# Small padding tiles in an encoder layer: every operand of TensorE at a multiple of 256 bytes

## The chip, the cores and the metric

One core of one Trainium2 chip. The metric is device time in microseconds (us) of one execution. The kernel before was timed three times; a fourth execution, under the hardware profiler, gave the trace that is read here.

## The reference

One encoder layer on x of 1024 rows by 1024 columns in float32, cut to what matters:

```python
h = rmsnorm(x, g_mix)
z = h @ w_in                                  # pooling channels | q | k | v
y_pool = pool_mixer(u_pool, w_pool_grp, pool_scale)
y_attn = diff_attention(q, k, v, ...)         # two softmax maps per head, block-causal chunks
gates = sigmoid(h @ w_gate + b_gate)
merged = gates[..., :D] * (y_pool @ w_branch_pool) + gates[..., D:] * (y_attn @ w_branch_attn)
x = x + merged @ w_out
h2 = rmsnorm(x, g_ffn)
x = x + square(relu(h2 @ w_up)) @ w_down
```

## The kernel before

All products run on TensorE. To keep float32 accuracy with a fast operand type, a float32 tile is split into a rounded high part and the rest (`split`, L127 on ScalarE, L128 on VectorE or GpSimd), and each product is three matmuls into the same PSUM bank, high by high, high by low and low by high (`mm3`, L133 to L135). Each matmul first loads a stationary operand of 128 columns (the profile's PEld), then streams a moving operand of 256, 384 or 512 columns. In the profile's names, `out<-in`, the first name behind the arrow is the moving operand and the second the stationary one: in `bp<-ypT,wbp`, ypT moves and wbp is loaded. The trace has 7601 matmuls: 7048 of `mm3` and of the score and sum products (L624, L625, L715, L716), which use the fast type, and 553 transposes against an identity tile (`identf`).

The work runs in stages. From about 30 to 700 us it makes q, k, v (`z`), scores (`sc`), transposed probabilities (`ta`), attention outputs (`po`), gates (`g`) and pooling channels (`u`), interleaved by a table of stages with steps (`ORDER`). From 700 to 910 us follow the branch products (`bp`, `ba`) and the output projection (`oX`, `oY`, `oZ`), from 910 to 1227 us the up projection (`X`, `Y`, `Z`, `W`), and to the end the down projection (`Da`, `Db`). The last three products are made by a scheme of seven half-size products (Strassen's), with sums on VectorE and GpSimd around them. TensorE takes its instructions in program order; each waits for semaphores of the engines that make its operands or free its bank.

SBUF tiles come from pools. A pool lays its tiles one behind the other in the order of first use, by bytes per partition, and the pools stand one behind the other; some pools (`side="right"`) are laid from the top end downwards. A tile of [128, n] float32 takes 4n bytes in each partition, rounded up to 32. The first tile of the kernel is `identf` (512 bytes), behind a reserved stretch and a few constants; then come `mhalf` (8 floats, 32 bytes), `ones` (512 bytes), `inv` and the small columns, and everything from the left end stands behind these. So the offset of a few small tiles within 256 bytes is passed on to all large tiles, which are multiples of 512 bytes. In the built program the matmuls' operands start, modulo 256 bytes, at:

| products | columns | matmuls | moving operand, before | stationary operand, before | both, after |
|---|---|---|---|---|---|
| `z` | 384 | 1536 | 96 | 96 | 0 |
| `g`, `u`, `bp`, `oX`, `oY`, `oZ`; `X`, `Z`, `W` over BT1, BT2, BT3, B22, BT4 | 512 | 2448 | 96 | 96 | 0 |
| `ba`; `X` and `Y` over B11, B21 | 512 | 768 | 224 | 96 | 0 |
| `Da`, `Db` | 512 | 1344 | 96 | 224 | 0 |
| `sc`, `po` over AT, `yp` | 256 to 512 | 888 | 224 | 224 | 0 |
| `po` over oqs | 256 | 64 | 160 | 160 | 0 |
| transposes `ta`, `tk`, `hps`, `hb` | 128 | 544 | 128 | 224 | 0 |
| nine small transposes (`trr`, `cols_ps`) | 128, 32 | 9 | 128 | 192, 128 | 0 moving; 32, 160 stationary |

Of the kernel before, what the change touches and what calls it, by code (L numbers as in the profile page):

```python
# [8 lines left out]
F32 = mybir.dt.float32  # L9
F32R = mybir.dt.float32r  # L10
# [7 lines left out]
P = 128  # L18
# [45 lines left out]
def encoder_kernel(  # L64
# [21 lines left out]
    nc = tc.nc  # L86
# [5 lines left out]
    const = ctx.enter_context(tc.tile_pool(name="const", bufs=1))  # L92
# [10 lines left out]
    fq = attn.enter_context(tc.tile_pool(name="fq", bufs=1))  # L103
    up = attn.enter_context(tc.tile_pool(name="up", bufs=N_U))
    ps_z = mix.enter_context(tc.tile_pool(name="ps_z", bufs=N_Z, space=PSUM))
    ps_f = mix.enter_context(tc.tile_pool(name="ps_f", bufs=N_F, space=PSUM))

    hcount = [0]

    def htile(shape, dt, name, th):  # L110
# [11 lines left out]
    def f(ap):  # L122
        return ap.bitcast(F32)

    def split(hi, lo, src, lo_eng=None):

        nc.scalar.copy(hi, src)  # L127
        return (lo_eng or nc.vector).tensor_tensor(lo, src, f(hi), op=ALU.subtract)  # L128

    def mm3(ps, lhs_hi, lhs_lo, rhs_hi, rhs_lo, first, last, more=False):  # L130

        kw = {"skip_group_check": True} if more else {}
        nc.tensor.matmul(ps, lhs_hi, rhs_hi, start=first, stop=False, **kw)  # L133
        nc.tensor.matmul(ps, lhs_hi, rhs_lo, start=False, stop=False, **kw)  # L134
        return nc.tensor.matmul(ps, lhs_lo, rhs_hi, start=False, stop=last, **kw)  # L135
# [103 lines left out]
        mp.append(m)  # L239


    identf = const.tile([P, P], F32, name="identf")
    make_identity(nc, identf)
    mhalf = const.tile([P, NT], F32, name="mhalf")
    nc.gpsimd.memset(mhalf, -0.5)
    ones = const.tile([P, P], F32R, name="ones")
    nc.gpsimd.memset(f(ones), 1.0)
    inv = const.tile([P, 16], F32, name="inv")
    for i in range(16):
        nc.gpsimd.memset(inv[:, i : i + 1], 1.0 / (i + 1))  # L250
# [1 line left out]
    cols = const.tile([P, 32], F32, name="cols")  # L252
    gs = const.tile([P, 1], F32, name="gs")
    zero = const.tile([P, 1], F32, name="zero")
    y_dram = dram.tile([D, S], F32, name="y_dram")
    r_dram = dram.tile([H, S], F32, name="r_dram")
    p_dram = dram.tile([POOLD, S], F32, name="p_dram")
# [150 lines left out]
    with ExitStack() as ph:  # L408
        sp = ph.enter_context(tc.tile_pool(name="sp", bufs=1))
# [4 lines left out]
        def s1(shape, dt, name, tag, bufs=1):  # L414
            return sp.tile(shape, dt, tag=tag, name=name, bufs=bufs)
# [274 lines left out]
        def stage_pv(h, p):  # L690
            V, views = KV[h][1], ATs.pop((h, p))[0]
            po = ps_o.tile([P, 512], F32, tag="o", name=f"po{h}_{p}")
            nkt = 2 * p + 2
            for kt in range(nkt):
                v = V[kt // 4]
                mm3(
                    po[:, 0:256], v[:, kt % 4, 0, :], v[:, kt % 4, 1, :],
                    views[kt][0], views[kt][1], kt == 0, kt == nkt - 1,
                )
                if kt % 2 and kt < nkt - 1:  # L700
                    yield
            oS = s1([P, 256], F32, f"oS{h}_{p}", "oS", 2)
            oq = s1([P, 256], F32, f"oq{h}_{p}", "oq")
            nc.scalar.activation(oq, po[:, 0:256], AF.Square)
            nc.scalar.copy(oS, po[:, 0:256])
            nc.scalar.dma_start(y_dram[h * P : (h + 1) * P, p * 256 : (p + 1) * 256], oS)
            oqs = s1([P, 2, 256], F32R, f"oqs{h}_{p}", "oqs")
            split(oqs[:, 0, :], oqs[:, 1, :], oq)
            st[h, p, "o"] = (po, oq, oqs)
            yield  # L710
# [34 lines left out]
        def stage(w, g):  # L745
            h, t = divmod(g, NT)
            if w == "A":
                if t == 0:
                    head_start(h)
                yield from stage_qkv(h, t)  # L750
            elif w == "B":
                yield from stage_prep(h, t)
            elif w == "C" and t % 2:
                yield from stage_qkT(h, t - 1)
            elif w == "D":
                yield from stage_scores(h, t)
            elif w == "E":
                yield from stage_aT(h, t)
            elif w == "F" and t % 2:
                yield from stage_pv(h, t // 2)  # L760
            elif w == "H" and t % 2:
                yield from stage_ssq(h, t // 2)
            elif w == "R" and t == NT - 1:
                yield from stage_norm(h)
            elif w == "W" and t == 0 and h:
                for kp in range(NK // 2):
                    load_w(h, kp)
                    split_w(h, kp, nc.gpsimd)
# [137 lines left out]
    def pool_of(stack, name, bufs, space=None, side=None):  # L906
        kw = {} if space is None else {"space": space}
        return stack.enter_context(
            tc.tile_pool(name=name, bufs=bufs, reuse_waits="tile", side=side, **kw)
        )  # L910

    hs = ctx.enter_context(ExitStack())
    norms = ExitStack()
    nb_pool = pool_of(hs, "nb", 4, side="right")
    pr1 = pool_of(hs, "pr1", N_R1, side="right")
    pr2 = [pool_of(hs, "pr20", 1, side="right")]
# [552 lines left out]
```

## Time and profile before

| | |
|---|---|
| median of 3 runs | 1545.42 us (1544.51 to 1545.88) |
| profiled execution | 1547.21 us, of which the span from first to last instruction 1545.4 us |
| granted TensorE clock | 1.000 |
| PE busy | 1527.3 us, 99% of the span, 7601 matmuls |
| PEld (stationary loads) busy | 1312.8 us, 85% |
| VectorE, ScalarE, GpSimd busy | 66%, 51%, 25% |
| DMA | 214.28 MB, mean 139 GB/s |

A matmul's record begins when it starts to fetch its moving operand and ends at a modelled time, so the records of consecutive matmuls overlap. What one matmul costs in a row of them is the time from its start to the start of the next, called its step below. A row of a group's answer gives first and last start and the count, from which the mean step follows; a window's count of matmuls in 100 us gives it too.

### The profile page before, as it was taken

The page shows a single profiled execution, that of the slowest core. Times are in us where ns is not written, and L with a number is a line of the kernel's source. Part 1 is how long each engine was busy: PE and PEld are TensorE (multiplying, and loading weights), DVE is VectorE, ACT ScalarE, POOL GpSimd, SP SyncE. Part 2 cuts the span into 40 slices and gives each one's busy share as a digit, 9 for nine tenths or more (in the row PEclk, how much of TensorE's full clock was granted, in tenths as well). Part 3 has the DMA queues.
Part 4 walks back from the last instruction along what each step waited for, and adds up shares of the span by engine and source line. Part 5 has one row for each costly group of instructions (what it writes and reads, how often), then busy time and mean ns, then how long its engine had stood idle before and what let it go on. Part 6 is the DMA issues. An engine that isn't in the chain of part 4 may idle for free.

```text
span 1545.4 us, 21680 instructions
## 1 busy us (share of the span) xinstructions
PE 1527.3 (99%) x7601; PEld 1312.8 (85%) x7601; DVE 1018.6 (66%) x2129; ACT 794.6 (51%) x1650; POOL 390.6 (25%) x469
## 2 busy tenths in 40 slices
PE   6999999999999999999999999999999999999999
PEld 6999999999999999888888887888888788888887
DVE  6777767677777778642635799667656677546662
ACT  6656555555555655544633477556555633333331
POOL 5434242434344343219637510000000000000000
PEclk9999999999999999999999999999999999999999
DMA  7112111111212121349736534555433899437650
GB/s 228 39 57 65 39 60 51 57 52 44 65 40 68 34 86 52 113 136 382 252 109 198 196 124 134 166 183 164 150 124 108 306 348 349 153 123 261 222 177 28
DMA packets 168568, 214.28 MB, mean 139 GB/s; under 512 B 10157, under 2 KB 104074, under 8 KB 168458
## 3 DMA queue, kind: packets, MB, share of 16 engines
q1 hardware_dynamic: 151050, 185.58, 36.2%
q10 hardware_dynamic: 17408, 27.30, 4.9%
q8 instruction: 60, 0.98, 0.3%
q14 instruction: 50, 0.41, 0.1%
HBM read 155.14 MB, written 57.70 MB: 138 GB/s over the span
## 4 chain that ended last, share of the span: by engine, by line
PE 93%; DVE 2%; DMA 2%; POOL 1%; ACT 1%; SPq 1%; issue 1%; ACTq 0%; POOLq 0%; DVEq 0%
PE z L135 6%; PE z L134 6%; PE z L133 6%; PE Da L134 4%; PE Da L135 4%; PE g L135 4%; PE Da L133 4%; PE g L134 4%; PE g L133 4%; PE Db L133 3%; PE Db L135 3%; PE Db L134 3%; PE X L133 3%; PE X L135 3%; PE X L134 3%; PE sc L624 2%
## 5 line engine op out<-in xcount | busy, mean ns | idle before, releaser
L135 PE MATMUL z<-wqkv,hT 128*128 128x384 f32 x512 | 173.8, 340 | 1.3 <-DVE hT L128 1.3
L133 PE MATMUL z<-wqkv,hT 128*128 128x384 f32 x512 | 174.8, 342 | 0.0
L134 PE MATMUL z<-wqkv,hT 128*128 128x384 f32 x512 | 174.2, 340 | 0.0
L635 ACT ACTIVATE s<-s,nm 128x256 f32<-128x256 f32 (+7 forms) x128 | 99.5, 778 | 73.8 <-DVE nm L627 70.7
L264 POOL TENSOR_TENSOR ms<-ms,mhalf 128x4 f32<-128x4 f32 x64 | 65.9, 1029 | 209.0 <-DVE ms L263 193.8
L133 PE MATMUL g<-hT,fwgate 128*128 128x512 f32 x256 | 101.0, 394 | 0.0
L135 PE MATMUL g<-hT,fwgate 128*128 128x512 f32 x256 | 100.6, 393 | 0.0
L134 PE MATMUL g<-hT,fwgate 128*128 128x512 f32 x256 | 100.5, 392 | 0.0
L135 PEld LDWEIGHTS z<-wqkv,hT 128*128 128x128 f32 x512 | 96.8, 189 | 3.3 <-DVE hT L128 2.4
L133 PEld LDWEIGHTS z<-wqkv,hT 128*128 128x128 f32 x512 | 96.9, 189 | 2.8 <-ACT hT L127 0.4
L134 PEld LDWEIGHTS z<-wqkv,hT 128*128 128x128 f32 x512 | 96.9, 189 | 1.7
L627 DVE CUSTOM_DVE_ANT_0 s<-sc,dist 128x512 f32<-128x512 f32 (+3 forms) x128 | 74.3, 585 | 23.5 <-PE sc L625 22.5
L624 PE MATMUL sc<-K,Q 128*128 128x512 f32 (+2 forms) x192 | 67.3, 356 | 0.4 <-DVE nm L627 0.4
L128 POOL TENSOR_TENSOR wqkv<-rqkv,wqkv 128x384 fp32r<-128x384 f32 x60 | 63.2, 1069 | 14.1 <-ACT wqkv L127 10.9
L625 PE MATMUL sc<-K,Q 128*128 128x512 f32 (+2 forms) x192 | 66.1, 349 | 0.0
L128 DVE TENSOR_TENSOR AS<-s,AS 128x512 fp32r<-128x512 f32 x64 | 43.4, 687 | 33.1 <-ACT AS L127 33.0
L128 POOL TENSOR_TENSOR fwgate<-frgate,fwgate 128x512 fp32r<-128x512 f32 x32 | 42.7, 1336 | 63.4 <-ACT fwgate L127 63.4
L135 PEld LDWEIGHTS g<-hT,fwgate 128*128 128x128 f32 x256 | 48.1, 188 | 9.6
L133 PEld LDWEIGHTS g<-hT,fwgate 128*128 128x128 f32 x256 | 48.1, 188 | 9.1 <-ACT go L382 0.2
L134 PEld LDWEIGHTS g<-hT,fwgate 128*128 128x128 f32 x256 | 48.1, 188 | 8.8
L135 PE MATMUL ba<-yT,wba 128*128 128x512 f32 x128 | 50.4, 395 | 0.0
L133 PE MATMUL ba<-yT,wba 128*128 128x512 f32 x128 | 50.4, 395 | 0.0
(458 smaller groups left out, 4595.4 us busy)
## 6 DMA issues: line engine op xcount, KB each, us to landing
wd<-in_w_down_dram SPq DMA_DIRECT2D x56, 512.0 KB, 5.4
wu<-in_w_up_dram SPq DMA_DIRECT2D x32, 512.0 KB, 5.1
udS<-us SPq DMA_DIRECT2D x64, 256.0 KB, 3.6
ur<-udS SPq DMA_DIRECT2D x32, 512.0 KB, 3.3
rqkv<-in_w_in_dram SPq DMA_DIRECT2D x64, 192.0 KB, 2.9
ur<-ud SPq DMA_DIRECT2D x24, 512.0 KB, 6.1
frgate<-in_w_gate_dram SPq DMA_DIRECT2D x32, 256.0 KB, 2.7
g_dram<-go ACTq DMA_DIRECT2D x32, 256.0 KB, 2.8
```

Of the source, the lines that this page charges most:

```text
L128: return (lo_eng or nc.vector).tensor_tensor(lo, src, f(hi), op=ALU.subtract)
L133: nc.tensor.matmul(ps, lhs_hi, rhs_hi, start=first, stop=False, **kw)
L134: nc.tensor.matmul(ps, lhs_hi, rhs_lo, start=False, stop=False, **kw)
L135: return nc.tensor.matmul(ps, lhs_lo, rhs_hi, start=False, stop=last, **kw)
L264: nc.gpsimd.tensor_tensor(dst, dst, mhalf[:, :n], op=ALU.pow)
L624: nc.tensor.matmul(dst, Q[:, i, 0, :], rhs, start=True, stop=False)
L625: nc.tensor.matmul(dst, Q[:, i, 1, :], rhs, start=False, stop=True)
L627: nc.vector.tensor_tensor_reduce(out=s[i][:, c : c + w], in0=sc[:, 0:w], in1=dist[:, o0 + c : o0 + c + w], scale=2.0 ** -(h + 1), scalar=B ...
L635: nc.scalar.activation(s[i][:, 0:n], s[i][:, 0:n], AF.Exp, bias=last, scale=-1.0, accum_out=Z[:, i, t : t + 1])
```

## The change

Five tiles that nothing reads or writes are allocated, to shift what stands behind them, and two small constants change places, so that the 512-byte tile comes ahead of the 32-byte one. The pads take 128 and 32 bytes in the pool of constants, 128 bytes in `fq` (the pool of the attention stage's wide tiles), 64 bytes in `sp` (its small tiles, at the place where `sp`'s tile list reaches the operands of the sum product), and 224 bytes at the right end, ahead of the pools of the output projection, the up and the down projection. After it 7592 of the 7601 matmuls have both operands at a multiple of 256 bytes, as the last column of the table shows. The tiles of the other engines and of the DMAs move by the same shifts: on VectorE 3769 operand places of the program were at 32 modulo 64 bytes and 934 at 0; after it 887 and 3816.

```diff
@@ encoder_kernel, the pools
+    def pad(pool_, n):
+        pool_.tile([P, n], F32, tag=f"pad{n}", name=f"pad{n}")
+
+    pad(fq, 32)
     hcount = [0]
@@ the constants
+    pad(const, 32)
     identf = const.tile([P, P], F32, name="identf")
     make_identity(nc, identf)
+    ones = const.tile([P, P], F32R, name="ones")
+    nc.gpsimd.memset(f(ones), 1.0)
     mhalf = const.tile([P, NT], F32, name="mhalf")
     nc.gpsimd.memset(mhalf, -0.5)
-    ones = const.tile([P, P], F32R, name="ones")
-    nc.gpsimd.memset(f(ones), 1.0)
@@
     zero = const.tile([P, 1], F32, name="zero")
+    pad(const, 8)
@@ stage_pv
             nc.scalar.dma_start(y_dram[h * P : (h + 1) * P, p * 256 : (p + 1) * 256], oS)
+            if not (h or p):
+                pad(sp, 16)
@@ after the attention pools are closed
     norms = ExitStack()
+    pad(pool_of(ctx, "edge", 1, side="right"), 56)
     nb_pool = pool_of(hs, "nb", 4, side="right")
```

The one place where instructions move is GpSimd's start, where it fills the constants. Before:

```order
masks.py:197 MEMSET identf 128x128
L245 MEMSET mhalf 128x8
L247 MEMSET ones 128x128
L250 MEMSET inv 128x1
masks.py:199 ISA
```

And now, with the lines numbered by the changed file:

```order
masks.py:197 MEMSET identf 128x128
L250 MEMSET ones 128x128
L252 MEMSET mhalf 128x8
L255 MEMSET inv 128x1
masks.py:199 ISA
```

The two fills have changed places, and GpSimd's first use of `mhalf` waits for a count of 3 instead of 2 on its own semaphore. TensorE, VectorE, ScalarE and the DMA queue of SyncE have the same instructions in the same order with the same waits as before.

## The prediction

> **What bounds the kernel now.** I read the page's first part, then TensorE's waits, then windows of 100 us.
>
> ```profile
> PE 1527.3 (99%) x7601; PEld 1312.8 (85%) x7601; DVE 1018.6 (66%) x2129; ACT 794.6 (51%) x1650; POOL 390.6 (25%) x469
> ```
>
> From all waits of TensorE (engine, line, releaser; us, times, longest), the four longest:
>
> ```profile
> PE hps L290 <- DVE hn L285: 9.5, 2, 9.0
> PE z L135 <- DVE hT L128: 1.3, 2, 1.1
> PE hps L290 <- DVE hT L128: 0.8, 1, 0.8
> PE oX L133 <- DVE mp L799: 0.6, 1, 0.6
> ```
>
> These make 12 us, all but 0.6 of it at the first tiles (`hps` and the first `z`); after that no other engine holds TensorE up. So the time is the sum of the steps from one matmul to the next, and what each step costs is the question. The windows (busy us and instructions of PE, PEld, DVE, ACT, POOL where present; clock; DMA share; GB/s):
>
> ```profile
> 100.00:200.00 100.00, 100.00 (x590) 92.61 (x589) 70.81 (x214) 58.26 (x147) 34.15 (x47) 1.00 0.17 52
> 700.00:800.00 100.00, 100.00 (x435) 81.47 (x435) 43.70 (x50) 48.85 (x77) 68.83 (x48) 1.00 0.76 267
> 1000.00:1100.00 100.00, 100.00 (x439) 82.04 (x439) 68.17 (x108) 60.20 (x109) 0.00 (x0) 1.00 0.52 167
> 1200.00:1300.00 100.00, 99.28 (x428) 79.96 (x427) 68.68 (x71) 46.77 (x58) 0.00 (x0) 1.00 0.92 329
> 1300.00:1400.00 100.00, 100.00 (x430) 80.43 (x430) 55.40 (x52) 36.04 (x36) 0.00 (x0) 1.00 0.49 170
> ```
>
> The clock is granted in full throughout. From 1300 to 1400 us only matmuls of 512 columns run, 430 of them: a step of 232.6 ns. The same shape has another step elsewhere, and that is the first thing to explain. From the answers on the tiles `bp` and `ba` (duration ns min/median/max, first and last start in us):
>
> ```profile
> L133 PE MATMUL bp<-ypT,wbp x64: 389/389/389, 700.0 to 742.9; 128*128 128x512 f32 x64
> L135 PE MATMUL bp<-ypT,wbp x64: 389/389/389, 700.5 to 743.3; 128*128 128x512 f32 x64
> L133 PE MATMUL ba<-yT,wba x128: 392/392/398, 743.6 to 832.5; 128*128 128x512 f32 x128
> L135 PE MATMUL ba<-yT,wba x128: 392/398/398, 744.0 to 832.9; 128*128 128x512 f32 x128
> ```
>
> `bp` is 192 matmuls from 700.0 to 743.3 us: 43.3/191 = 226.7 ns a step. `ba` is 384 from 743.6 to 832.9: 89.3/383 = 233.2 ns. Shape, clock and types are equal, and neither waits. What differs in the program is where the operands start: `bp` has both at 96 modulo 256 bytes, `ba` has its moving operand at 224 and its stationary one at 96. In the list of groups nearly every one with equal offsets outside the attention stage has a mean of 389 to 392 ns, and every one with offsets 128 apart 394 to 398:
>
> ```profile
> L135 PE MATMUL oX<-wo,A 128*128 128x512 f32 x64 | 24.9, 389 | 0.0
> L133 PE MATMUL Z<-B22h,AS 128*128 128x512 f32 x64 | 24.9, 389 | 0.0
> L133 PE MATMUL Y<-B21h,A 128*128 128x512 f32 x64 | 25.4, 397 | 0.0
> L133 PE MATMUL Da<-w_2h,u_2h 128*128 128x512 f32 x32 | 12.6, 395 | 0.0
> ```
>
> So addresses reach TensorE's pace. I take that as shown; how far it goes is not.
>
> **The change, part by part.** Nothing is added to any engine: the pads are never touched. GpSimd's two fills change places ahead of the first transposes, which wait 9 us for VectorE's `hn` anyway (the row above); that costs nothing, and without this cover it would be the time of a fill of 8 floats.
>
> First term, the unequal offsets. They belong to 384 (`ba`), 384 (`X` and `Y` over B11 and B21), 768 (`Da`) and 576 (`Db`) matmuls, 2112 together. After the change all are equal, as `bp`'s are now: 2112 × (233.2 − 226.7) = 13.7 us. TensorE's queue is the path, so it counts in full.
>
> Second term, what is left in `bp`'s step. To split it I need other widths; from the timeline of PE, a run of `po` with 256 columns, its first and last, 22 steps apart, and a run of `z` with 384, 8 steps up to the first `g`:
>
> ```profile
> 674.18 0.28 PE L134 MATMUL po<-AT_0l,V 128*128 128x256 f32 x1
> ...
> 676.81 0.28 PE L135 MATMUL po<-AT_4h,V 128*128 128x256 f32 x1
> ```
>
> ```profile
> 319.97 0.34 PE L134 MATMUL z<-wqkv,hT 128*128 128x384 f32 x1
> ...
> 321.36 0.39 PE L133 MATMUL g<-hT,fwgate 128*128 128x512 f32 x1
> ```
>
> 2.63/22 = 119.5 ns at 256 columns, 1.39/8 = 173.8 at 384, 226.7 at 512. From 256 to 512 columns the step grows by 107.2 ns, 0.419 ns a column; taken off, 12 to 13 ns remain at all three widths. So each matmul of the fast type carries about 13 ns that don't depend on its length, while both its operands start at an odd multiple of 32 bytes. Is that the offset's doing, or the price of passing from one matmul to the next? The nearest rows in which the moving operand starts at a multiple of 128 bytes are the transposes, whose identity is at 128:
>
> ```profile
> 123.50 1.03 PE L680 MATMUL ta<-identf,s 128*128 128x128 f32 x8
> 124.29 0.36 PE L624 MATMUL sc<-K,Q 128*128 128x256 f32 x1
> 124.49 0.28 PE L625 MATMUL sc<-K,Q 128*128 128x256 f32 x1
> 124.61 0.28 PE L624 MATMUL sc<-K,Q 128*128 128x256 f32 x1
> ```
>
> The record after the transposes begins early, so I count to the one behind it: from 123.50 to 124.49 lie eight transposes and one `sc`, whose own step is 120 (124.49 to 124.61): 870/8 = 109 ns each. If a column of their slower type takes twice 0.419 ns, which I can only infer, 128 take 107 and 2 ns remain, not 13, although their stationary operand starts at 224. That speaks for the moving operand's offset. Nor does the stationary load's size matter: behind the last head a transpose with 8 stationary columns (its load takes 83 ns where others take 188) is loaded under a `g`, and that `g`'s step stays 220 to 230 ns:
>
> ```profile
> L736 PEld LDWEIGHTS trr<-identf,r x8: 83/83/84, 144.7 to 690.4; 128*8 128x8 f32 x8
> ...
> 690.38 0.39 PE L133 MATMUL g<-hT,fwgate 128*128 128x512 f32 x1
> 690.60 0.27 PE L736 MATMUL trr<-identf,r 128*8 128x128 f32 x1
> ```
>
> The bounds of this term are 0 (a fixed price) and 13 ns (all of it the offset). I take 11, the remainder less the transposes' 2, since theirs is the only row with an aligned moving operand: 7048 × 11 = 77.5 us.
>
> The Trainium skill ("TensorE: Matmul & The Clock Gate", section "Back-to-back issue gap") gives a warm step of N/2.4 + 2.5 ns. That is 215.8 at 512 columns where this trace has 226.7 at best, and 10.9 × 7048 would be 76.8 us.
>
> Third term, new waits. The other engines' work does not shrink, unless their tiles' new places help them, which no row shows; their waits cost TensorE 12 us at most now, so I price that at 0 to a few us either way. Where TensorE's cover is thin I take a share back. DMA is 92% busy from 1200 to 1300 us (the row above): 428 matmuls there lose up to 17.5 ns each, 7.5 us, and 92.5 us leave no slack for 92 us of DMA: I take 3. Two stretches of the chain that ended last lie off TensorE, each from the first to the last of its pieces (start us, length):
>
> ```profile
> 819.36 0.63 ACT wo L127
> ...
> 865.78 0.61 DVE mp L799
> 912.01 0.87 ACT y L1021 x3
> ...
> 940.56 0.61 DVE BT1l L128
> ```
>
> That is 47 and 29 us of other engines' and DMA work which just meets TensorE. If TensorE covers them 6% faster, 3 and 2 us appear as waits. In the attention stage VectorE is 71 us busy of 100; 94 would still hold that, and I allow 2. Together 10 us.
>
> The sum for the profiled execution: 1547.2 − 13.7 − 77.5 + 10 = 1466.0 us. The median of the timed runs is 1.8 below that execution: 1464.
>
> **The rivals.** (a) Only equal offsets count, and the 13 ns are the price of passing to the next matmul: the term of 77.5 is nothing. For it: the remainder is the same for `z` at offset 96 and `po` at 224, and a constant needs no memory to explain it. Against it: the transposes. 1547.2 − 13.7 − 1.8 = 1532.
>
> (b) Half of the remainder goes, because one of the two operands' offsets makes a part of it: 38.8 + 13.7 less 5 of waits, 1498.
>
> (c) No change: the steps of `bp` and `ba` differ by something else in their stages, such as DMA or evacuation. The groups above, the same in four stages, are against it. 1545.4. The Trainium skill ("SBUF — State Buffer", section "Specifications (TRN2)") has lines of 16 bytes, and by that rule 32, 96, 160 and 224 are starts of lines already, so nothing would be gained; `ba` against `bp` does not agree.
>
> (d) Slower: with every operand at offset 0, the moving stream, the next stationary load and the other engines' accesses start in the same place of the memory at the same time, and meet. The dearest step in these rows is `ba`'s slower record, 398 against `bp`'s 389. If all steps go there, 4936 matmuls pay 9 ns and 2112 pay 2.5 more than their mean: 44.4 + 5.3 = 49.7 us, 1595. It decides once the mean step over all 7048 rises by 2 ns (13.7/7048) above `bp`'s level. Against it: equal offsets are the cheaper case in every group above.
>
> **How the numbers follow.** The forecast (the remainder gone to 9 to 13 ns) 0.56; (b) 0.13; (a) 0.16; (c) 0.08; (d) 0.07. The likeliest case alone runs from 1450 (13 ns, 7048 × 13 = 91.6 instead of 77.5) to 1482 (9 ns and a few more waits). The range goes up to 1538, (a) with half of its gain, and so takes in (a) and (b); it leaves out (c), (d) and a little below 1450, under 2 in 10. A difference of 0.2%, 3 us, is about what the three runs' spread can tell. All of the forecast, (a) and (b) are faster by more: 0.85; (c) is the same: 0.08; (d) slower: 0.07.
>
> **What would show it.** Right: the count of matmuls from a window inside the down projection rises from 430 to some 460 in 100 us and that of `bp`'s steps falls to about 216 ns; `bp` and `ba` have one mean; `po` near 109 and `z` near 163; transposes stay at 109. Wrong in the second term: `bp` stays at 226.7 with `ba` joining it (a), or stops between 217 and 225 (b). Wrong in the third: PE's waits grow past 20 us, at `oX` behind `wo`, at `Da` behind `w_0h` or `w_0l`, or anywhere in the attention stage. Wrong altogether: `bp`'s step above 227.

## The result, and the profile after

| | before | after |
|---|---|---|
| median of five runs, same chip | 1545.42 us | 1532.73 us |
| ratio | | 0.9924, interval 0.9905 to 0.9942 |
| profiled execution (span) | 1547.21 (1545.4) us | 1532.49 (1530.7) us |

The change makes the kernel 12.7 us faster. I had forecast 81. The number is that of rival (a), 1532, in which only the difference of the two offsets counts and nothing of the 13 ns goes.

The page's first part of the changed kernel, and the window inside the down projection:

```profile
PE 1513.4 (99%) x7601; PEld 1314.4 (86%) x7601; DVE 1027.9 (67%) x2129; ACT 794.7 (52%) x1650; POOL 390.1 (25%) x469
1300.00:1400.00 100.00, 100.00 (x443) 82.85 (x442) 56.82 (x54) 36.39 (x37) 0.00 (x0) 1.00 0.49 170
```

TensorE is still the bound, and 443 matmuls stand in the window where 430 stood. A window counts about two records that only reach into it, so I read steps from a window as 100 us over the count less two, good to about 0.5 ns: 226.8 ns here, 233.6 before. The answers on `bp` and `ba` (lines 137 to 139 are 133 to 135 of before):

```profile
L137 PE MATMUL bp<-ypT,wbp x64: 388/390/390, 699.8 to 742.6; 128*128 128x512 f32 x64
L139 PE MATMUL bp<-ypT,wbp x64: 388/390/390, 700.2 to 743.1; 128*128 128x512 f32 x64
L137 PE MATMUL ba<-yT,wba x128: 388/390/390, 743.3 to 829.6; 128*128 128x512 f32 x128
L139 PE MATMUL ba<-yT,wba x128: 388/390/390, 743.7 to 830.1; 128*128 128x512 f32 x128
```

`bp` keeps its step: 43.3 us over 191, 226.7 ns, although both its operands moved from 96 to 0. `ba` fell to it: 86.8 over 383, 226.6 ns. The groups of other stages, from the list, show the same meeting at one mean:

```profile
L139 PE MATMUL oX<-wo,A 128*128 128x512 f32 x64 | 24.9, 389 | 0.0
L137 PE MATMUL Z<-B22h,AS 128*128 128x512 f32 x64 | 24.9, 389 | 0.0
L137 PE MATMUL Y<-B21h,A 128*128 128x512 f32 x64 | 25.1, 392 | 0.0
L137 PE MATMUL Da<-w_2h,u_2h 128*128 128x512 f32 x32 | 12.5, 389 | 0.0
L686 PE MATMUL ta<-identf,s 128*128 128x128 f32 x288 | 44.9, 272 | 0.0
```

`Y` and `Da` had 397 and 395; the transposes' 272 is unchanged. So is their step. The same eight of them in the changed kernel:

```profile
123.32 1.04 PE L686 MATMUL ta<-identf,s 128*128 128x128 f32 x8
124.11 0.36 PE L630 MATMUL sc<-K,Q 128*128 128x256 f32 x1
124.31 0.28 PE L631 MATMUL sc<-K,Q 128*128 128x256 f32 x1
124.43 0.28 PE L630 MATMUL sc<-K,Q 128*128 128x256 f32 x1
```

From 123.32 to 124.31, less one `sc` of 120 ns, are 870 ns, 109 each as before, although their operands were 96 bytes apart (128 and 224) and now both start at 0. Behind the first tiles no wait of TensorE is longer than 0.8 us; its four longest are:

```profile
PE hps L296 <- DVE hn L291: 8.9, 1, 8.9
PE hps L296 <- DVE hT L132: 1.2, 1, 1.2
PE X L137 <- ACT BT2h L131: 0.8, 1, 0.8
PE z L139 <- DVE hT L132: 0.7, 2, 0.5
```

So the gain is where the prediction's first term put it, and the second term's 77.5 us are absent. The experiments ask two things: is it the difference of the offsets alone that counts, and whose are the 13 ns that stayed?

### The profile page after: what moved, and what is told of

It reads as the page before. It is cut to its first block, busy times and chain, and to the rows that moved or that the text cites. A ratio compares the mean times of both kernels' runs of the same rounds, so it can differ in the third digit from the quotient of the medians.

```text
span 1530.7 us, 21680 instructions
## 1 busy us (share of the span) xinstructions
PE 1513.4 (99%) x7601; PEld 1314.4 (86%) x7601; DVE 1027.9 (67%) x2129; ACT 794.7 (52%) x1650; POOL 390.1 (25%) x469
## 4 chain that ended last, share of the span: by engine, by line
PE 97%; DVE 2%; DMA 0%; issue 0%; ACT 0%; SPq 0%; POOL 0%; ACTq 0%; POOLq 0%
PE z L139 6%; PE z L137 6%; PE z L138 6%; PE g L139 4%; PE g L138 4%; PE g L137 4%; PE Da L138 4%; PE Da L139 4%; PE Da L137 4%; PE Db L137 3%; PE Db L139 3%; PE Db L138 3%; PE X L139 3%; PE X L137 3%; PE X L138 3%; PE sc L630 2%
```

## Experiments

**One pad, no multiple of 256.** The kernel before with one line more (`pad` is the helper of the changed kernel):

```diff
+    pad(pool_of(ctx, "edge", 1, side="right"), 32)
     nb_pool = pool_of(hs, "nb", 4, side="right")
```

> The kernel before with one pad alone: 128 bytes at the right end, so that the tiles there move from 224 to 96 modulo 256 and meet the others' 96. 1728 matmuls (X and Y over B11 and B21, Da, Db) become equal at 96; ba's 384 stay 128 bytes apart; nothing is at a multiple of 256. If only the difference of the two offsets counts: 1545.4 - 1728 x 6.5 ns = 1534, Da and Db at 226.7 ns a step, ba at 233. If a start at a multiple of 256 is what pays: no change, 1545, Da and Db at 233.

Measured: 1535.25 us (median of four runs) against 1545.05 of the kernel before beside it, ratio 0.9938 (0.9921 to 0.9954). Its window and its `ba`:

```profile
1300.00:1400.00 100.00, 100.00 (x443) 82.80 (x442) 56.51 (x54) 37.04 (x37) 0.00 (x0) 1.00 0.52 172
L136 PE MATMUL ba<-yT,wba x128: 392/392/398, 743.5 to 832.4; 128*128 128x512 f32 x128
L138 PE MATMUL ba<-yT,wba x128: 392/398/398, 744.0 to 832.9; 128*128 128x512 f32 x128
```

The down projection has the step of the changed kernel with both operands at 96; `ba`, left apart, keeps its 233 ns (89.4 over 383).

**All equal at 96.** The same with a second pad of 128 bytes, the changed kernel's own ahead of the attention tiles:

```diff
+    pad(fq, 32)
...
+    pad(pool_of(ctx, "edge", 1, side="right"), 32)
     nb_pool = pool_of(hs, "nb", 4, side="right")
```

> The kernel before with two pads of 128 bytes, at the right end and ahead of the attention stage's tiles: every matmul of the fast type but the 64 sum products has both operands at 96 modulo 256, none at 0. If only the difference counts: the same time as the changed kernel, 1532 to 1533, all steps of 512 columns at 226.7. If the multiple of 256 has a share of its own: slower than the changed kernel by that share, up to 1545.

Measured: 1533.54 us (median of four runs) against 1545.05, ratio 0.9926 (0.9911 to 0.9940); the changed kernel's 0.9924 lies in this interval. `ba`:

```profile
L137 PE MATMUL ba<-yT,wba x128: 389/389/389, 743.5 to 829.8; 128*128 128x512 f32 x128
L139 PE MATMUL ba<-yT,wba x128: 389/389/389, 743.9 to 830.3; 128*128 128x512 f32 x128
```

86.8 over 383 again. A multiple of 256 has no share of its own that can be measured; two pads do what five and an exchange do.

**Other distances.** The changed kernel with the right end's pad made shorter, so that one operand of 1728 matmuls moves away from 0: by 64 bytes (`edge` of 40 floats), 32 (48) and 128 (24).

```diff
-    pad(pool_of(ctx, "edge", 1, side="right"), 56)
+    pad(pool_of(ctx, "edge", 1, side="right"), 40)
```

> The changed kernel with 160 bytes instead of 224 at the right end: 1728 matmuls (X and Y over B11 and B21, Da, Db) have operands 64 bytes apart instead of equal. If any difference modulo 256 costs what 128 bytes did: Da and Db at 233 ns a step, 1544. If only a difference of 128 bytes collides: 226.7 as now, 1532.5. If two equal starts are themselves a collision and make the 13 ns remainder: below 226.7, down to 216, and 1514.

> The changed kernel with 192 bytes instead of 224 at the right end: Da, Db and X, Y over B11, B21 have operands 32 bytes apart. If any unequal pair pays 6.5 ns: Da and Db at 233, 1544. If the price goes by the 64-byte or 128-byte place: 32 bytes apart costs nothing, 227 and 1532.5.

> The changed kernel with 96 bytes instead of 224 at the right end: Da, Db and X, Y over B11, B21 are again 128 bytes apart, now at 0 and 128 instead of 96 and 224. If only the difference counts: 233.3 ns a step in alternating steps near 229 and 238, as in the kernel before, 1544. If a start at 128 is as good as one at 0: 226.7 and 1532.5.

Measured, one run each: 1547.23, 1545.15 and 1544.80 us. The windows, in the order 64, 32, 128; first:

```profile
1300.00:1400.00 100.00, 100.00 (x430) 80.12 (x430) 55.66 (x52) 36.04 (x36) 0.00 (x0) 1.00 0.50 171
```

then:

```profile
1300.00:1400.00 100.00, 100.00 (x430) 80.50 (x429) 54.25 (x50) 35.26 (x36) 0.00 (x0) 1.00 0.49 167
```

and:

```profile
1300.00:1400.00 100.00, 100.00 (x432) 81.04 (x432) 54.83 (x51) 35.63 (x37) 0.00 (x0) 1.00 0.49 170
```

Steps of 233.6, 233.6 and 232.6 ns. Every distance tried costs 5.8 to 6.8 ns on average over the 226.8 of equal offsets, whether 32, 64 or 128 bytes, and the hope that some distance takes the 13 ns away fell with it. A start at 128 is hardly better than one at 32 or 64 when the other operand is at 0, and the two alternating steps expected there did not come back: start to start, the trace has steps spread from 228 to 241. That the period is 256 bytes and not 512 follows from `ba` in the changed kernel: there its moving operand and the next stationary one lie an odd multiple of 256 bytes apart in the built program, at 226.6 ns.

**The 2-byte type.** The changed kernel with the down projection's parts in bfloat16, in tiles of the old size, so that addresses stay; first run once, then timed.

```diff
-            hi, lo = (pool_.tile([P, 2, 512], F32R, tag="op", name=f"{n}{j}_{q}{x}") for x in "hl")
-            split(hi, lo, src, dve)
+            hi, lo = (
+                pool_.tile([P, 2, 1024], mybir.dt.bfloat16, tag="op", name=f"{n}{j}_{q}{x}")[:, :, 0:512] for x in "hl"
+            )
+            nc.scalar.copy(hi, src)
+            nc.vector.tensor_tensor(lo, src, hi, op=ALU.subtract)
```

> The changed kernel with the down projection's operands (Da, Db) in a 2-byte type at the same addresses (high and low parts rounded to bfloat16, so the result is coarser). If the 13 ns remainder is the price of passing from any matmul to the next: steps stay at 226.7 ns, 443 matmuls in 100 us. If it belongs to the 4-byte type: steps near 216, 1344 x 11 ns = 15 us less, 1518.

> The kernel of the first look at the 2-byte type again, now timed: the changed kernel with Da's and Db's operands in bfloat16. By that look 1518, 15 us or 1.0% below the changed kernel; if the look was chance, 1532.

Measured: 1518.17 us in the single run; timed, 1518.09 us (median of four runs) against 1545.22 of the kernel before, ratio 0.9822 (0.9805 to 0.9838), faster than both kernels, at the price of coarser parts. The timed kernel's windows, and its longest wait in the down projection:

```profile
1200.00:1300.00 100.00, 99.07 (x454) 52.43 (x454) 75.92 (x76) 46.80 (x57) 0.00 (x0) 1.00 0.96 355
1300.00:1400.00 100.00, 100.00 (x466) 45.30 (x464) 58.91 (x56) 39.37 (x40) 0.00 (x0) 1.00 0.55 186
PE Da L137 <- ACT w_0h L1376: 0.7, 1, 0.7
```

100/464 is 215.5 ns a step: 11 of the remainder's 12 to 13 ns go with the type, at the same addresses and 512 columns. The Trainium skill's formula ("TensorE: Matmul & The Clock Gate", section "Back-to-back issue gap") gives 215.8 for it and agrees; for the 4-byte type this trace is 11 ns above the formula. That section calls the formula the gap of an isolated matmul and gives about 131 ns for a stream of loads and matmuls at 512 columns; no run here comes near that (215.5 is the lowest), though every matmul here has its own load. The first window shows a DMA share of 0.96 with 454 matmuls in it, 438 in the changed kernel's, and TensorE's longest wait in the down projection is 0.7 us.

The same exchange in the kernel before, where the operands are 128 bytes apart:

> The kernel before with the down projection's operands in the 2-byte type at the same addresses, 128 bytes apart (96 and 224; the result is coarser). If unequal offsets cost a 2-byte stream too: Da and Db near 222 ns a step. If the 2-byte type is free of it: 216, the time 1545 - 1344 x 17.4 ns = 1522.

Measured: 1522.62 us in one run.

```profile
1300.00:1400.00 100.00, 100.00 (x466) 45.34 (x464) 59.50 (x57) 39.22 (x40) 0.00 (x0) 1.00 0.57 188
```

215.5 ns: the 2-byte type doesn't mind the distance. So both prices, the 11 ns and the 6.5, go with the fast 4-byte type. The transposes, of the plain 4-byte type, don't show the second: they kept 109 ns when their operands moved from 96 bytes apart to none. With the type the bytes of the moving stream are halved and the loads get shorter (45.30 us over 464, 98 ns each, against 187); of these only the length of the load was tried by itself, next.

**Shorter loads.** In the changed kernel and in the kernel before, the stationary load cut to 32 columns in all but the first matmul of a sum, and once to 64. The rows that a matmul writes are cut with its load:

```diff
-                mm3(
-                    banks[t], uh[:, i, c], ul[:, i, c], wh[:, i, :], wl[:, i, :],
...
+                n = P if first else 32
+                c = slice(t * P, t * P + n)
...
+                nc.tensor.matmul(banks[t][0:n], uh[:, i, c], wh[:, i, :], start=first, stop=False, **kw)
+                c = slice(t * P, t * P + 32)
+                nc.tensor.matmul(banks[t][0:32], uh[:, i, c], wl[:, i, :], start=False, stop=False, **kw)
+                nc.tensor.matmul(banks[t][0:32], ul[:, i, c], wh[:, i, :], start=False, stop=q == NQ - 1 and i == 1, **kw)
```

> The changed kernel with the same cut of the down projection's stationary loads to 32 columns, all offsets 0. If the 11 ns that the 4-byte type pays above the 2-byte type come from its stationary load, they shrink with it: 227 to about 219 ns a step, 1522. If they belong to the moving stream: 227 and 1532.5 as now.

> The kernel before with the down projection's stationary loads cut from 128 to 32 columns, but for the first matmul of each sum (three quarters of the output rows are then left out); moving operands, addresses (96 and 224) and count stay. If the 6.5 ns of unequal offsets come from the load meeting the moving stream, they shrink with the load to about 1.6 ns; if the offset costs once per matmul, Da and Db keep 233 ns a step and the time stays 1545.

> The changed kernel with the down projection's stationary loads cut to 64 columns, 256 bytes, but for the first matmul of each sum (half of the output rows are left out). If what counts is that load and moving stream keep the same place modulo 256 bytes, a load of 256 bytes keeps it and the step stays 226.7, where one of 128 bytes made 231.6. If any shorter load disturbs: 229 to 232.

Measured, one run each: 1540.05, 1543.04 and 1538.33 us. The windows; equal offsets with 32 columns:

```profile
1300.00:1400.00 100.00, 100.00 (x433) 47.35 (x432) 54.11 (x51) 35.99 (x36) 0.00 (x0) 1.00 0.50 166
```

offsets 128 bytes apart with 32 columns:

```profile
1300.00:1400.00 100.00, 100.00 (x435) 47.27 (x434) 54.91 (x51) 36.34 (x38) 0.00 (x0) 1.00 0.51 170
```

equal offsets with 64 columns:

```profile
1300.00:1400.00 100.00, 100.00 (x436) 58.55 (x435) 54.74 (x52) 36.01 (x36) 0.00 (x0) 1.00 0.50 169
```

The loads got shorter (47.35 us over 432 is 110 ns each, 58.55 over 435 is 135, against 82.85 over 442, 187, with 128 columns), but the steps are 232.0, 230.9 and 230.4 ns. Of the cases expected only one came true, that any shorter load disturbs: with equal offsets it costs about 4 to 5 ns more, not less, and 256 bytes of it don't save the step. With unequal offsets it gains some 3 of the 6.5. So neither price shrinks in proportion to the load, the 11 ns that bfloat16 saves do not come from its shorter load alone, and among the cases tried the cheap 226.7 needs both equal offsets and a load of 128 columns.

**A shorter stream.** The changed kernel with 480 of 512 moving columns:

```diff
-                mm3(
...
+                n = 512 if first else 480
+                nc.tensor.matmul(banks[t][:, 0:n], uh[:, i, c], wh[:, i, 0:n], start=first, stop=False, **kw)
+                nc.tensor.matmul(banks[t][:, 0:480], uh[:, i, c], wl[:, i, 0:480], start=False, stop=False, **kw)
+                nc.tensor.matmul(banks[t][:, 0:480], ul[:, i, c], wh[:, i, 0:480], start=False, stop=q == NQ - 1 and i == 1, **kw)
```

> The changed kernel with the down projection's moving operands cut from 512 to 480 columns, 1920 bytes, no multiple of 256 (but for the first matmul of each sum; 32 of 512 columns of the output are left out). If the 13 ns are the same at any length and the moving stream's end doesn't matter: 226.7 - 32 x 0.417 = 213.4 ns a step. If the stream's end must meet the 256-byte place too: 218 to 220, half of the saving gone.

Measured: 1524.35 us in one run.

```profile
1300.00:1400.00 100.00, 100.00 (x463) 86.41 (x463) 60.62 (x58) 38.93 (x39) 0.00 (x0) 1.00 0.55 186
```

100/461 is 216.9 ns, between 213.4 and the 218 to 220 of the other case. Start to start, the trace has mostly two kinds of steps, near 213 and near 221, in about equal numbers. So neither case holds for every matmul: about half pay some 8 ns more than the others, and why those is not shown.

## Why the prediction was wrong

**The first term was right.** 2112 × 6.5 ns = 13.7 us stood against 12.7 in the medians and 14.7 in the profiled executions. The steps in question fell to `bp`'s level, and the pad at the right end alone gave 9.8 us where its 1728 matmuls make 11.2 by the same price.

**The second term was the step that failed.** The 13 ns that every matmul keeps at any width were put down to odd starts, with the transposes as the row with an aligned moving operand: 2 ns there, hence 11 to gain. Their step was read rightly (109 ns, unchanged with every operand at a multiple of 256), though its split into 107 and 2 was inferred and no run tests it. The comparison was the fault: they differ from the other matmuls in being transposes and in their type as well as in their offset, and I let the offset carry all of the difference. `bp` moved from 96 to 0 at both operands and kept 226.7 ns. The bfloat16 runs keep the addresses, change the type with its bytes, and step at 215.5 ns whether the offsets are equal or not. So the term was 0, its lower bound. Rival (a), at 0.16, was right in the time and in the offsets; its reading of the 13 ns as the price of passing to the next matmul holds for the 1 or 2 ns that bfloat16 keeps, not for the 11. The rows did hold the hint that the prediction named for (a): the remainder was the same for `z` at 96 and `po` at 224.

One more reading failed, though no number hung on it: that the stationary load's size doesn't matter rested on one step read to 10 ns, and loads cut to 32 and 64 columns made the step 5.2 and 3.6 ns longer.

**The third term was too large where it was tested.** I took 10 us back for waits that a TensorE faster by 6% would uncover. The change's own gain was too small to test that, but the bfloat16 kernel quickens the very stage for which I took 3, to a DMA share of 0.96, and no long wait followed: of the 14.8 us (1344 × 11 ns) 14.4 arrived, the gain of 27.1 over the kernel before that was timed beside it less the changed kernel's 12.7. The other places stay untried.

**Rivals (b), (c) and (d)** found no support in the runs. For (c) the Trainium skill's lines of 16 bytes ("SBUF — State Buffer", section "Specifications (TRN2)") would make all these offsets equal; two operands 32 bytes apart cost 6.8 ns here (233.6 less 226.8), so for TensorE's two streams the measurement decides otherwise. In (d) all starts in one place were to collide; equal starts are the cheapest case here.

What stays open is the mechanism. The price of unequal offsets depends on where the moving operand and the stationary one stand to each other modulo 256 bytes, on the fast 4-byte type, and, not in proportion, on the load's length. Which of the two streams waits for the other was not shown, nor where the 11 ns come from.

## What to carry to other kernels

Where TensorE is the bound and its operands are of the fast 4-byte type, see that the moving and the stationary tile start at the same offset modulo 256 bytes: here two pads of 128 bytes gave 0.7%, and 32 bytes too few at the right end lost it again (1545.15 us in one run). Before a remainder is put down to one property, look for a row, or make a run, that changes this property alone: my nearest row differed in three. The fast 4-byte type's own 11 ns weigh more than the addresses: over all 7048 matmuls they would make 77.5 us by my estimate, against 13.7, though only the down projection's 1344 were tried, at the price of coarser parts. No placement tried removes them.

## What the runs showed of the hardware that was not expected

- A step of 512 columns takes 226.7 ns in the fast 4-byte type with equal offsets modulo 256 bytes, about 233 with any distance tried (32, 64, 128), and 215.5 in bfloat16, with equal offsets and with 128 bytes between them.
- The transposes, in the plain 4-byte type, step at 109 ns with operands 96 bytes apart and with both at 0.
- A shorter stationary load can make the step longer: 232.0 ns with 32 columns and 230.4 with 64, against 226.7 with 128, all with equal offsets.
